# One hybrid layer on one core: the delta-rule phase issued in a TensorE order that the kernel's source works out

## The chip, the core and the metric

The kernel runs on one core of a Trainium2 chip. A core has a matrix engine (TensorE; PE in the profile, with its weight loads as PEld), VectorE (DVE), ScalarE (ACT), GpSimd (POOL) and SyncE (SP), each with an instruction stream of its own that it works off in order; semaphores connect them. SBUF is the working memory with 128 partitions; PSUM takes TensorE's results and has eight banks of 128 x 512 fp32. The metric is the time of one execution on the device, in microseconds (us). Of the kernel before, three runs took 1362.74, 1362.84 and 1366.62 us, so the median is 1362.84 us.

## The reference

512 tokens of width 1024 go through one layer with two mixing branches and an MLP. The first branch is the gated delta rule (8 heads, keys of 128, values of 256):

```
xn = rmsnorm(x); proj = xn @ w_in
q, k, v = split(silu(causal_depthwise_conv(proj[qkv], conv_a)))      # 4 taps over time
q = l2norm(q) / sqrt(128); k = l2norm(k); beta = sigmoid(.); g = -exp(a_log) * softplus(. + dt_bias)
# per head and chunk:
decay  = exp(g_cum[i] - g_cum[j])  for i >= j, else 0
lower  = strict_lower((k * beta) k^T * decay);  T = inverse(1 + lower)
attn   = (q k^T) * decay
v_new  = T (v * beta) - T (k * beta * exp(g_cum)) @ state
o      = (q * exp(g_cum)) @ state + attn @ v_new
state  = state * exp(g_last) + (k * exp(g_last - g_cum))^T @ v_new
ya = (rmsnorm(o, norm_a) * silu(z)) @ w_br_a
```

The second branch is chunked retention (rotary q and k, fixed decays, a silu gate, `w_br_b`). Both are gated and summed, go through `w_out`, and the MLP `square(relu(x @ w_up)) @ w_down` follows, with an rmsnorm before and after each part.

## The kernel before

All large products are fp32-accurate by splitting: a weight block `raw` of 128 x 1024 is loaded by SP (`weights`, L88), ACT rounds it to `whi` (L117), VectorE forms `wlo = raw - whi` (L118), and TensorE does three products for each pair of tiles: whi·xhi, whi·xlo, wlo·xhi (`mm3`, L84 to L86). One such product is a matmul of 128 x 128 by 128 x 512 (512 columns streamed). A "product" below is a group of these that fills one or more PSUM banks: `feature_major` (L252, features on partitions) and `token_major` (L272).

The delta-rule phase (L545 to L954) handles 8 heads in four pairs `g2`, with chunks of 128 tokens (the reference's 64-token chunks give the same function). Its pieces:

- `keys(g4)` (L683), four heads at a time: product K, then `conv_silu` (L630): ACT copies PSUM to `c_raw` (L635) and makes the first tap (L640), VectorE adds three taps (L642), ACT does tanh (L643), VectorE the last multiply (L646). TensorE transposes the result to token rows (`to_tokens`, L649), ACT sums squares (L657). `decays` (L659) makes the 128 x 128 decay tile: eight ACT scalings of a triangle (L665), two TensorE products against the constant matrix `later` (L666), one exp (L668). It is called for every head twice, once in `keys` and once in `values_queries`. Gram products k·kᵀ (L710) are scaled into `mt` (L713, which lies in `acc`), and `kd` is scaled (L716).
- `base_inverse(g4)` (L720): the 32 x 32 diagonal blocks of 16 matrices are rearranged through DRAM (L726, L732) onto 64 partitions and inverted there by 31 steps of a VectorE multiply (L741) and subtract (L747), each on at most 256 elements; results go back through DRAM (L749 to L753). It runs twice, for the two groups of heads.
- `double_blocks` (L758): four levels of small TensorE products that grow inverses from 32 to 128, called four times for 8 matrices each.
- `values_queries(g2)` (L804): products V and Q, convolutions, `vt` (L811), the attention tiles `at` (L830, L832), masked on POOL (L836).
- `recurrence(g2)` (L846): for four chunks in order: ks (L862), the correction (L865), px (L871), `vn` by ACT (L875), pc (L880), the new state (L885/L890), qs (L894), its scaling (L896), po (L901), the sum (L903). Each step takes one of three PSUM banks of the tag `dl`.
- `gated(g2)` (L927): product Z, tanh (L604), two VectorE multiplies (L605, L607); `gated_features` (L609) transposes the gated rows through the one PSUM bank of the tag `tr`; `ya_partial` (L671) multiplies by `w_br_a`.

The order on every engine is made when the program is built: a scheduler with a cost model takes instructions in program order and priority (`high_priority` moves them ahead). What `keep_in_program_order` marks stays in the order of the source. In the kernel before that is true of a part of the start and of the second branch's `token_product` (L242); the delta-rule products are free, and the scheduler mixes them. `add_blocks` (L158) puts DRAM-to-DRAM additions for later weights on POOL's queue, and `copy_block` puts copies on SP's.

## Time and profile before

| | |
|---|---|
| median of 3 runs | 1362.84 us |
| profiled execution, first to last instruction | 1362.5 us |
| start (norm of x, first keys) | to about 42.5 us |
| delta-rule phase | 42.5 to 485.5 us |
| second branch and its gates | to about 960 us |
| mixing and MLP | to the end |

The phases' bounds are read from the trace's timeline: the first product of the second group of keys starts at 42.57 us, the last sum of `ya_partial(2)` (L678) at 485.3 us. In the profile a TensorE instruction's start is exact and its end is modelled, so that neighbours overlap in the rows: the distance from one start to the next is what an instruction takes of the engine. An fp32 product that is not split shows as two records.

### The profile page before, as it was taken

What the parts mean: (1) busy time and instruction counts of PE and PEld (TensorE: products, weight loads), DVE (VectorE), ACT (ScalarE), POOL (GpSimd) and SP (SyncE); (2) the same over time, 40 slices, a digit from 0 to 9 for tenths busy, and PEclk for the clock granted to TensorE, in tenths of its full rate; (3) what the DMA queues carried; (4) which work ended last, traced back from release to release, by engine and by line L of the source; (5) the groups of instructions that cost most, each with busy time, mean ns of one, the idle gap of its engine ahead of it and who ended that gap; (6) DMA issues with size and microseconds to landing.
All of it is one profiled execution on the core that took longest, in us unless ns stands there. A gap on an engine that the chain in (4) does not pass through costs nothing.

```text
span 1362.5 us, 17876 instructions
## 1 busy us (share of the span) xinstructions
PE 1347.0 (99%) x6685; PEld 1110.7 (82%) x6685; DVE 912.8 (67%) x1606; ACT 651.7 (48%) x1204; POOL 109.4 (8%) x161
## 2 busy tenths in 40 slices
PE   9999999999999999999999999999999999999997
PEld 7888787788877888888888888888889888888886
DVE  5799899864665557567477577575775744828535
ACT  5977564624543322453453343343355736436441
POOL 2010310121011002000000100011101100000000
PEclk9999999999999999999999999999999999999999
DMA  5254715379458447775584782488639843625421
GB/s 178 64 154 133 202 43 180 117 153 238 108 124 169 110 147 158 190 240 193 131 255 132 192 263 93 154 217 182 199 117 238 224 154 110 197 95 169 132 86 62
DMA packets 101718, 214.70 MB, mean 158 GB/s; under 512 B 7158, under 2 KB 20624, under 8 KB 101120
## 3 DMA queue, kind: packets, MB, share of 16 engines
q1 hardware_dynamic: 85616, 170.41, 39.1%
q0 software_dynamic: 15280, 42.03, 17.0%
q8 instruction: 52, 0.85, 0.3%
q10 hardware_dynamic: 736, 1.12, 0.2%
q14 instruction: 34, 0.28, 0.1%
HBM read 207.77 MB, written 64.49 MB: 200 GB/s over the span
## 4 chain that ended last, share of the span: by engine, by line
PE 89%; DVE 5%; DMA 2%; ACT 2%; issue 1%; DVEq 0%; ACTq 0%
PE mm L84 18%; PE mm L85 18%; PE mm L86 18%; PE mm L242 10%; PE dl L242 10%; PE tr L323 3%; PE mm L456 2%; DVE wlo L118 1%; PE dl L86 1%; PE dl L85 1%; PE dl L84 1%; PE dl L901 1%; PE dl L871 1%; DVE c_y L642 1%; PE dl L880 1%; PE dl L862 1%
## 5 line engine op out<-in xcount | busy, mean ns | idle before, releaser
L118 DVE TENSOR_TENSOR wlo<-raw,whi 128x1024 fp32r<-128x1024 f32 x245 | 298.8, 1221 | 269.0 <-ACT whi L117 267.7
L117 ACT CAST whi<-raw 128x1024 fp32r<-128x1024 f32 x245 | 257.4, 1052 | 428.9 <-PE mm L85 243.4
L84 PE MATMUL mm<-actT,whi 128*128 128x512 f32 x480 | 190.1, 396 | 0.0
L85 PE MATMUL mm<-actT,whi 128*128 128x512 f32 x480 | 189.9, 396 | 0.0
L86 PE MATMUL mm<-actT,wlo 128*128 128x512 f32 x480 | 189.0, 395 | 0.0
L84 PEld LDWEIGHTS mm<-actT,whi 128*128 128x128 f32 x480 | 90.2, 188 | 18.7 <-ACT c_y L640 0.8
L86 PE MATMUL mm<-hn,wlo 128*128 128x512 f32 (+1 forms) x288 | 105.4, 366 | 0.0
L85 PE MATMUL mm<-hn,whi 128*128 128x512 f32 (+1 forms) x288 | 105.3, 366 | 0.0
L84 PE MATMUL mm<-hn,whi 128*128 128x512 f32 (+1 forms) x288 | 105.3, 366 | 0.0
L86 PEld LDWEIGHTS mm<-actT,wlo 128*128 128x128 f32 x480 | 90.3, 188 | 17.9
L85 PEld LDWEIGHTS mm<-actT,whi 128*128 128x128 f32 x480 | 90.3, 188 | 17.8
L84 PE MATMUL mm<-og,whi 128*128 128x512 f32 x256 | 99.7, 390 | 1.0 <-DVE zz L605 1.0
L85 PE MATMUL mm<-og,whi 128*128 128x512 f32 x256 | 99.6, 389 | 0.0
L86 PE MATMUL mm<-og,wlo 128*128 128x512 f32 x256 | 99.6, 389 | 0.0
L242 PE MATMUL mm<-whi,xsum 128*128 128x512 f32 x256 | 80.8, 389 | 0.0
L642 DVE SCALAR_TENSOR_TENSOR c_y<-c_raw,convw,c_y 128x512 f32<-128x512 f32 x96 | 69.7, 743 | 2.4 <-ACT c_y L640 1.8
L85 PEld LDWEIGHTS mm<-hn,whi 128*128 128x128 f32 x288 | 54.3, 189 | 8.8
L84 PEld LDWEIGHTS mm<-hn,whi 128*128 128x128 f32 x288 | 54.3, 189 | 8.7
L86 PEld LDWEIGHTS mm<-hn,wlo 128*128 128x128 f32 x288 | 54.3, 189 | 8.7
L84 PE MATMUL mm<-whi,actT 128*128 128x512 f32 x152 | 61.1, 402 | 0.1
L242 PE MATMUL dl<-whi,actT 128*128 128x512 f32 x192 | 61.1, 389 | 0.0
L242 PE MATMUL dl<-whi,ffq 128*128 128x512 f32 x192 | 61.0, 389 | 0.0
(345 smaller groups left out, 2608.8 us busy)
## 6 DMA issues: line engine op xcount, KB each, us to landing
raw<-in_w_in_dram SPq DMA_DIRECT2D x101, 512.0 KB, 4.3
raw<-sums SPq DMA_DIRECT2D x56, 512.0 KB, 4.2
raw<-in_w_up_dram SPq DMA_DIRECT2D x36, 512.0 KB, 4.6
sums<-in_w_in_dram SPq DMA_DIRECT2D x32, 512.0 KB, 5.6
sums<-sums POOLq DMA_DIRECT2D x28, 512.0 KB, 7.1
raw<-in_w_down_dram SPq DMA_DIRECT2D x26, 512.0 KB, 3.8
sums<-in_w_down_dram SPq DMA_DIRECT2D x24, 512.0 KB, 7.4
raw<-in_w_br_a_dram SPq DMA_DIRECT2D x16, 512.0 KB, 4.0
```

The costliest lines, as they stand in the source:

```text
L84: nc.tensor.matmul(ps, lh, rh, start=first, stop=False)
L85: nc.tensor.matmul(ps, lh, rl, start=False, stop=False)
L86: nc.tensor.matmul(ps, ll, rh, start=False, stop=last)
L117: nc.scalar.copy(hi[:, :n], raw[:, :n])
L118: nc.vector.tensor_tensor(lo[:, :n], raw[:, :n], hi[:, :n], ALU.subtract)
L242: m = nc.tensor.matmul(pss[t], lhs[i // 2], rhs[i % 2], start=first and k + i == 0, stop=k + i == 5, skip_group_check=not first,)
L323: nc.tensor.transpose(ps, src, ident)
L456: nc.tensor.matmul(ps[:, ts], ws[w][:, kk, f * P : (f + 1) * P], xs[x][:, k, ts], start=first and kk + i == 0, stop=kk == len(ks) - 1 and ...
L642: nc.vector.scalar_tensor_tensor(y, raw[:, j : j + T], tap(j), y, ALU.mult, ALU.add)
L862: nc.tensor.matmul(ks[:, hh, :], kf[:, h0 + hh, cs], state[:, hh, :], start=True, stop=True)
L871: nc.tensor.matmul(px[:, hh, :], rt[:, nn[hh], :], vx[:, hh, :], start=True, stop=True)
L880: nc.tensor.matmul(pc[:, hh, :], kd[:, nn[hh], :], vn[:, hh, :], start=True, stop=True)
```

## The change

The arithmetic of the layer stays; the delta-rule phase is rewritten.

1. **Order.** A class `Clock` adds up assumed TensorE times. Each piece is a generator; `run` steps those that are due by this clock and fills the rest with units of three 512-column matmuls from a list of large products. All TensorE instructions of the phase are pinned in that order.
2. **Decays once.** Cumulated g goes as 32 rows to DRAM and comes back broadcast over 128 partitions; POOL masks it, ACT makes 32 exps into `dall`, which `keys` and the attention tiles both use (and which the attention tiles then replace).
3. **Convolution from PSUM.** The copy to `c_raw` is left out; the taps read PSUM. Values and queries take one ACT `Silu` in place of tanh and a VectorE multiply. The gates take `Silu` too, also in the second branch.
4. **Inverse once.** All 32 matrices on 128 partitions, moved by VectorE block transposes in place of DRAM; each step's two operations are cut in two halves. All keys come before it, and doubling runs for all four groups level by level.
5. `kd` is no longer scaled: ACT writes px twice, scaled by `brd` and by `br`. qs moves next to ks, and the state is updated in place.

```diff
+SMALL_US, CONV_US, TOK_US, PK_US, INV_US, DB_US = 10.5, 6.5, 2.5, 2.0, 62.0, 0.5
+VT_US, KS_US, PX_US, PC_US, GATE_US, ... = 2.5, 2.4, 3.5, 2.4, 11.0, ...
+# INV_PRIO 0, CONV_PRIO 600, SMALL_PRIO 800, KEY_PRIO 600, DECAY_US 20.0, AHEAD 700
...
+    class Clock:
...
+        def matmul(self, *args, **kwargs):
+            m = tc.keep_in_program_order(nc.tensor.matmul(*args, **kwargs))
...
+            if args[1].dtype == F32R:
+                self.now += 0.0135 + n / 2400
+            else:
+                self.now += 0.006 + 4 * n / 2400
...
+        def run(self, fillers):
...
+                due = [c for c in self.chains if self.ready(c[0]) <= self.now]
+                if due:
+                    self.step(min(due, key=lambda c: self.ready(c[0])))
+                    continue
...
+                        if all(self.events.get(n, float("inf")) <= self.now for n in f[1]):
+                            fillers.remove(f)
+                            current = f[0]()
+                            break
...
+        clock.matmul(pg[0:32, 2, :], gf, tri, start=True, stop=True)
...
+        nc.gpsimd.dma_start(g_d, g_rows)
...
+            nc.gpsimd.dma_start(gb.rearrange("p n t -> p (n t)"), rows.partition_broadcast(P))
+            nc.gpsimd.affine_select(gb, gb, pattern=[[0, 16], [1, P]], ...)
...
+                        nc.scalar.activation(
+                            dall[:, 4 * h + c, :], gb[:, 4 * i + c, :], AF.Exp, bias=neg_g[:, c, h : h + 1]
...
+            clock.done(f"decay{g4}", DECAY_US + 5 * g4)
...
-        nc.scalar.copy(raw[:, 3 : T + 3], ps)
...
+                nc.vector.scalar_tensor_tensor(y[:, s:T], ps[:, 0 : T - s], tap(j), y[:, s:T], ALU.mult, ALU.add)
+            if th is None:
+                with tc.issue_after(exps[-1].ins):
+                    nc.scalar.activation(y, y, AF.Silu, scale=2.0)
...
+        def base_inverse():
+            yield "mt0"
+            yield "mt1"
...
+                    cuts = (0, (nr + 1) // 2, nr) if nr > 3 else (0, nr)
...
+            clock.done("inverse", INV_US)
...
+                    qs = chain_bank()
+                    for hh in range(2):
+                        clock.matmul(qs[:, hs[hh], :], qf[:, hh, cs], state[:, hs[hh], :], start=True, stop=True)
+                    yield KS_US - (clock.now - t1)
...
+                    for w, scale in ((vx, brd), (vn, br))[c == 3 :]:
+                        for hh in range(2):
+                            nc.scalar.activation(w[:, hs[hh], :], px[:, hs[hh], :], AF.Copy, scale=scale[:, nn[hh] : nn[hh] + 1])
+                yield PX_US
...
+        def delta_chain():
+            yield "inverse"
+            yield from double_blocks()
+            for g2 in range(4):
+                for f in range(4):
+                    yield f"v{g2}{f}"
+                yield f"q{g2}"
+                yield from recurrence(g2)
+                clock.start(gate_chain(g2))
...
+                (second_keys_filler, ()),
+                (value_filler(0), ()),
+                (query_filler(0), ()),
+                (gate_filler(0), ()),
+                (value_filler(1), ()),
+                (query_filler(1), ()),
+                (ya_filler(0), ("og0", "doubled")),
+                (value_filler(2), ("og0",)),
+                (query_filler(2), ("og0",)),
+                (gate_filler(1), ("gate0",)),
...
```

At the start, half of the first keys' products for the second 256 tokens move ahead of the second half of the small product (beta and g), pinned. `AHEAD` raises the priority of weight splits within the phase.

## The prediction

> **What bounds the kernel now.** I read the page first, then the stretches before and after 485.5 us, then TensorE's waits, then the chain of waits, and last the groups on VectorE and ACT.

> ```profile
> span 1362.5 us, 17876 instructions
> PE 1347.0 (99%) x6685; PEld 1110.7 (82%) x6685; DVE 912.8 (67%) x1606; ACT 651.7 (48%) x1204; POOL 109.4 (8%) x161
> ```

> ```profile
> 42.50:485.50 443.00, 437.72 (x2411) 354.10 (x2410) 325.84 (x730) 238.62 (x587) 57.18 (x96) 1.00 0.54 138
> 485.50:560.00 74.50, 74.50 (x343) 61.77 (x342) 53.65 (x66) 26.48 (x33) 9.21 (x11) 1.00 0.67 163
> 600.00:625.00 25.00, 25.00 (x112) 20.68 (x112) 19.50 (x27) 13.22 (x21) 0.00 (x0) 1.00 0.95 306
> ```

> ```profile
> 578.23 5.44 PE dl L242 x24
> ```

> A matmul of 512 columns takes 5.44 / 24 = 0.227 us, and a 25 us stretch that touches 112 of them is full. After the delta-rule phase TensorE is saturated, and only work taken from it shortens the time there. So everything is decided in the 443.0 us of the phase. Its TensorE work, by start-to-start distances:

> ```profile
> 42.50:485.50 443.00, 178.55 (x449) 84.24 (x449) 1.00 0.54 138
> 42.50:485.50 443.00, 12.08 (x32) 5.63 (x32) 1.00 0.54 138
> 42.50:485.50 443.00, 28.23 (x180) 20.76 (x180) 1.00 0.54 138
> 171.69 1.03 PE L894 MATMUL dl<-st,qf 128*128 128x256 f32 x4
> 172.55 1.03 PE L901 MATMUL dl<-vn,at 128*128 128x256 f32 x4
> 98.20 0.60 PE L323 MATMUL tr<-cmat,qf 128*128 128x128 f32 x4
> 98.64 1.06 PE L830 MATMUL dl<-qf,kf 128*128 128x128 f32 x8
> 99.45 0.71 PE L666 MATMUL dl<-tg,later 128*128 128x512 f32 x2
> 100.00 0.39 PE L84 MATMUL mm<-actT,whi 128*128 128x512 f32 x1
> 158.60 1.07 PE dl L797 x16
> 184.86 1.09 PE L780 MATMUL dl<-rn,acc 32*32 32x32 f32 x32
> ```

> The first row is L84 alone; L85 and L86 have 448 each, so 1345 x 0.227 = 304.9. Decays (second row): 32 x 0.227 = 7.3. Transposes (third row): 180 x 0.11 = 19.8. Recurrence: 272 records at 0.86 / 4 = 0.215, 58.6. Gram and attention: 128 at 0.81 / 8 = 0.101, 13.0. Doubling: 128 records at 0.067 and 320 at 0.032, 18.8. Sum 422.4, so some 20 us of 443.0 are not work. The order can win no more than that. The view of TensorE's waits in the phase has six rows of one wait each, 5.0 us together (first two and last):

> ```profile
> PE dl L880 <- ACT vn L875: 1.2, 1, 1.2
> PE tr L594 <- issue: 1.1, 1, 1.1
> ...
> PE dl L666 <- DVE acc L713: 0.5, 1, 0.5
> ```

> The other 15 are short breaks, mostly at changes between kinds of matmul.

> **The change, part by part.**

> *Decays once.* Gone are 32 products of 0.227 us, 7.3, and the breaks around 16 pairs of them. From 99.45 to 100.00 a pair takes 0.55 us instead of 0.453, so 0.1 each, 1.6. One cumulative product is added, 0.2. Net -8.7 us of TensorE. ACT loses the 128 scalings:

> ```profile
> L665 ACT ACTIVATE tg<-cmat,ghi 128x128 fp32r<-128x128 f32 x64 | 22.5, 403 | 0.3 <-PE dl L666 0.3
> L836 POOL TENSOR_SCALAR_AFFINE_SELECT at<-at 128x1024 f32<-128x1024 f32 x4 | 7.6, 1892 | 27.2 <-DVE ssq L842 15.6 <-DVE at L832 11.6
> ya_d<-acc POOLq DMA_DIRECT2D x2, 1024.0 KB, 9.3
> vecs_in<-in_norm_b_dram POOLq DMA_DIRECT2D x1, 8.0 KB, 2.2
> ```

> The new path is longer: 2.2 us for a small transfer, up to 9.3 for 1 MB, 2 x 1.89 for a mask of twice the size, 16 exps of 0.403: 21.7 us to the first half, where the planner says 20; the second half, with one more mask and 16 exps, about 32 against 25. The second keys and first values (192 matmuls, 43.5 us) cover it. Without that cover the Gram scalings, and behind them the inverse, are late by up to 7 us. Two queues get a new wait. On POOL the mask waits for the broadcast; behind it stand only the inverse's memsets, which need the keys anyway. On ACT the exps wait for the mask; behind them stand weight splits, and three split blocks are held at a time, each good for 24 matmuls or 5.4 us, so a hold-up of up to 10 us stays covered. The first values' taps write into the tile that the broadcast used, so V's first two PSUM banks are held until the last exp; the other two take its second half. I take 0 for all of it; bounds 0 and 7.

> *Convolution, gates, kd.*

> ```profile
> L642 DVE SCALAR_TENSOR_TENSOR c_y<-c_raw,convw,c_y 128x512 f32<-128x512 f32 x42 | 30.4, 742 | 0.5 <-ACT c_y L640 0.5
> L605 DVE SCALAR_TENSOR_TENSOR zz<-zz,mm 128x512 f32<-128x512 f32 x16 | 10.8, 678 | 0.3 <-ACT zz L604 0.3
> ```

> VectorE loses the last multiply (L646; like L605 over 512 elements, 0.68 us) for 24 tiles, 16 gate multiplies (L605), 32 kd scalings and one of two inverses; ACT loses 30 copies. Both only feed TensorE, so I book nothing. A tap from PSUM is not in the trace; the nearest rows are L605, which reads PSUM, at 0.678 and L642, all in SBUF, at 0.742: bounds 0.68 and 0.74 a tap, and I keep 0.74. Gone with the inverse are POOL's transfers for it (L726 to L765); the block additions on that queue stay 10 and 12 in the phase. In the second branch 16 VectorE multiplies go; TensorE is full there: 0. Table loads for `Silu` lie on ACT, at 48%: 0, and a few us if each met a wait. The start is reordered between products that stood close to each other: 0, plus or minus 1.

> [...]

> *The pinned order.* It replaces the order in which the six waits stood. All six lie at places where the new order puts products between, so -5.0; none of the 15 us of breaks is booked, since each chain step is still a visit between large products. At best a third, 5, goes too; at worst they grow by as much.

> *Inverse once, late.* This is the part that can cost. TensorE has work before the first recurrence: K, V, Q, Z, V, Q are 480 matmuls, 108.8 us; 80 transposes 8.8; Gram and attention 9.7; doubling 18.8: 146 us. VectorE's work in the same time:

> ```profile
> L118 DVE TENSOR_TENSOR wlo<-raw,whi 128x1024 fp32r<-128x1024 f32 x17 | 20.7, 1218 | 9.5 <-ACT whi L117 9.3
> L713 DVE SCALAR_TENSOR_TENSOR acc<-dl,br,dt 128x128 f32<-128x128 f32 x32 | 10.9, 344 | 0.0
> L747 DVE TENSOR_TENSOR mrb<-mrb,tmp 64x31 f32<-64x31 f32 (+15 forms) x31 | 10.2, 330 | 0.1
> L741 DVE TENSOR_TENSOR tmp<-mrb 64x31 f32<-64x31 f32 (+15 forms) x31 | 10.2, 328 | 0.1
> L748 DVE COPY mrb<-mrb 64x1024 f32<-64x1024 f32 x1 | 1.1, 1131 | 0.0
> L782 DVE COPY y<-dl 32x256 f32<-32x256 f32 x8 | 3.4, 424 | 3.6 <-PE dl L780 3.5
> L303 DVE SCALAR_TENSOR_TENSOR rs_y<-rs_t,rs_y 128x8 f32<-128x8 f32 (+1 forms) x30 | 4.9, 163 | 0.6
> 85.66 2.06 DVE L642 SCALAR_TENSOR_TENSOR c_y<-c_raw,convw,c_y 128x512 f32<-128x512 f32 x3
> ```

> 40 splits 48.7; 20 convolutions of three taps, eight with the last multiply of 0.68, 50.0; Gram scalings, rescaled values and attention 19.2; the inverse 20.4, some 4 for its halves (an estimate: the 62 more instructions at the 0.07 us that neighbours leave between them) and 11 block transposes at 1.1 (not in the trace; nearest row L748), 36.5; doubling's 28 copies at 0.42 (L782) to 0.69, 14; some 50 small operations at 0.16 (L303), 8: 176. Three taps took 2.06 us rather than 2.23, so VectorE delivers it in 176 x 0.92 = 163 us. That is 17 more than TensorE's 146. But V and Q of the second pair, 19.5 x 0.92 = 18 of it, are not needed by the first recurrence and can follow the inverse. So TensorE waits between 0 and 17 us at the first doubling product; I take 2.5, nearer to 0 since the work that can stand back is as large as the gap.

> *Recurrence 0 without cover.* The next products wait for its gated rows (`og0`, `gate0`), and the six above are used up. Before, it ran so:

> ```profile
> 163.75 1.02 PE L871 MATMUL dl<-vt,rt 128*128 128x256 f32 x4
> 165.34 1.13 PE L880 MATMUL dl<-vn,kd 128*128 128x256 f32 x4
> 183.91 1.03 PE L901 MATMUL dl<-vn,at 128*128 128x256 f32 x4
> 172.75 0.84 ACT L896 ACTIVATE vt<-dl,eg 128x256 f32<-128x256 f32 x2
> ```

> From 163.75 to 184.8 are 21.0 us, of which 17 groups of 0.86 are its own, 14.7: 6.3 us that other products filled before and nothing must fill now. The second pair's queries leave a few pieces there, so 3.0; bounds 0 and 6.3.

> Sum, on the profiled execution: 1362.5 - 8.7 - 5.0 + 2.5 + 3.0 = 1354.3; the median stands 0.3 above the span, 1354.6 us. Its own range: 1354.6 - 2.5 - 3.0 - 5 = 1344 with nothing late and a third of the breaks gone; 1354.6 + 3.3 + 2 = 1360 with recurrence 0 bare and the inverse a little late.

> **Rivals.**

> *The inverse becomes the bound (slower).* Place: the first doubling product. Convolutions and splits carry priority 600 and 700, the inverse 0; if VectorE does all of V and Q first, the whole 17 us are waited, and recurrence 0 behind it is bare: 1354.6 + 14.5 + 3.3 = 1372. It decides against the change once the wait passes 2.5 + 8.2 = 10.7 us. For it: VectorE was that full while the first inverse ran before (48.97 of 50 us, the row below). Against it: the planner leaves 62 us for the inverse, and the rows give 36.5 for it alone.

> ```profile
> 100.00:150.00 50.00, 48.95 (x254) 39.65 (x253) 48.97 (x143) 39.05 (x116) 9.17 (x15) 1.00 0.58 174
> ```

> *po waits for a bank (no change).* With qs held from ks on, po of chunks 1 and 2 may get the bank of qs. Its scaling writes where pc reads, so it starts after pc (0.86), takes 0.84 and a hand-over: about 1.1 us of waiting in eight places, 8.8: 1363. For it: three banks and five tiles for each chunk. Against: px's bank is free by then, if the scheduler takes that one.

> *The planner's clock doesn't fit (slower).* Its latencies are fixed, and a pinned TensorE cannot step aside as the free order could. With some 110 visits, 0.15 us more at each is 16: 1354.6 + 16 = 1371. Against: most of its gaps are longer than the rows ask (3.5 us where px to pc took 1.59, from 163.75 to 165.34).

> **How the numbers follow.** Forecast 0.54, inverse 0.22, bank 0.14, clock 0.10. About 0.3%, 4 us, can be told from no change. The forecast is faster by that except at its upper end (0.04 within): faster 0.50. Within: 0.04, plus 0.12 of the bank rival: 0.16. Slower: the rest, 0.34. The range starts at 1344 and reaches into both slow cases, to 1374; above lies what stalls in both ways at once.

> **What would show it.** Right: no L666 rows; TensorE's waits in the phase under 10 us; the phase's end near 477 instead of 485.5; waits concentrated at the first doubling and the first recurrence. Wrong: a wait of over 10 us at doubling behind VectorE's inverse; eight waits at po behind ACT's scaling of qs; a TensorE idle share spread over all transposes; or times after 485.5 us that differ, which nothing here explains.

## The result and the profile after

The changed kernel takes 1387.24 us (median of four runs, 1373.68 to 1398.07) against 1363.67 us; the ratio is 1.0088, with a 95% interval of 1.0061 to 1.0115: slower, where faster was forecast. This ratio and those below leave out runs over 1.5% above the fastest of the same kernel, here the two above 1395 us, whose mean granted clock was 0.977 and 0.979. The profiled run has 1373.68 us and a span of 1371.9. Its page begins:

```profile
span 1371.9 us, 17419 instructions
PE 1346.9 (98%) x6655; PEld 1111.1 (81%) x6655; DVE 879.5 (64%) x1491; ACT 608.9 (44%) x1085; POOL 81.5 (6%) x91
```

TensorE is busy for as long as before (1347.0), although 32 products are gone. VectorE and ACT lost 33 and 43 us. Two of the stretches shown of before, now after (start and end, length, then busy time and count of PE, PEld, DVE, ACT and POOL, granted clock, DMA share, GB/s), with two of 25 us inside the phase:

```profile
42.50:485.50 443.00, 429.85 (x2376) 354.51 (x2376) 302.33 (x641) 199.73 (x474) 30.52 (x30) 0.99 0.53 135
600.00:625.00 25.00, 25.00 (x111) 20.49 (x110) 17.17 (x22) 13.15 (x21) 0.00 (x0) 1.00 0.96 296
100.00:125.00 25.00, 21.49 (x92) 17.36 (x91) 23.53 (x47) 8.15 (x11) 2.85 (x3) 0.93 0.78 203
150.00:175.00 25.00, 20.81 (x139) 16.34 (x137) 24.00 (x21) 7.68 (x10) 2.87 (x3) 0.86 0.90 224
```

Two stretches stand out: TensorE stands still for 3.5 and 4.2 us while VectorE is full, and the granted clock is below 1.00, which it was in none of the stretches shown of before. The first product of the second branch marks the end of the phase; from the timeline, before and then after:

```profile
578.07 0.39 PE L242 MATMUL dl<-whi,actT 128*128 128x512 f32 x1
```

```profile
577.64 0.39 PE L244 MATMUL dl<-whi,actT 128*128 128x512 f32 x1
```

So the phase gained 0.4 us where 8 were forecast, and the part behind it, which the change hardly touches, lost 9.8 (1371.9 - 577.6 against 1362.5 - 578.1). A second profile of each kernel (e0_before and e0_after below) gives 576.48 and 578.37, so the phase's 0.4 is uncertain by one or two microseconds; the loss behind it, 11.6 there, is not in doubt. These are two separate questions.

**Inside the phase.** TensorE's waits there (what waited, for what, us in all, times, longest):

```profile
PE tr L583 <- ACT vt L806: 4.4, 2, 4.2
PE dl L583 <- ACT vt L806: 3.5, 1, 3.5
PE dl L574 <- ACT vt L1094: 1.6, 2, 1.0
PE dl L574 <- ACT vn L1094: 0.9, 2, 0.6
```

All rows of this view add up to 13.0 us; before it was 5.0.

The two long waits stand at token transposes of V, at 109.6 and 158.9 us, and the releaser is the Silu of V. ACT was not late itself: its input was. VectorE's timeline ahead of the first wait (start, duration), a little shortened:

```profile
97.98 0.75 DVE L803 SCALAR_TENSOR_TENSOR vt<-mm,convw,vt 128x511 f32<-128x511 f32 x1 [0.26 <-ACT vt L800]
98.65 2.03 DVE L908 STREAM_TRANSPOSE mrb<-acc 32x1024 f32<-32x1024 f32 x1
100.62 0.69 DVE L803 SCALAR_TENSOR_TENSOR vt<-mm,convw,vt 128x510 f32<-128x510 f32 x1
101.34 2.02 DVE L908 STREAM_TRANSPOSE mrb<-acc 32x1024 f32<-32x1024 f32 x1
...
105.96 2.03 DVE L908 STREAM_TRANSPOSE mrb<-acc 32x1024 f32<-32x1024 f32 x1
108.02 0.75 DVE L803 SCALAR_TENSOR_TENSOR vt<-mm,convw,vt 128x510 f32<-128x510 f32 x1
108.80 1.97 DVE L908 STREAM_TRANSPOSE mrb<-acc 32x1024 f32<-32x1024 f32 x1
110.80 1.22 DVE L120 TENSOR_TENSOR wlo<-raw,whi 128x1024 fp32r<-128x1024 f32 x1
111.94 0.74 DVE L803 SCALAR_TENSOR_TENSOR vt<-mm,convw,vt 128x509 f32<-128x509 f32 x1
```

Between V's taps stand the inverse's block transposes, at 2.0 us each and not at the 1.1 that the prediction took. The groups of all eleven:

```profile
L908 DVE STREAM_TRANSPOSE mrb<-acc 32x1024 f32<-32x1024 f32 x4 | 8.0, 2012 | 0.1
L933 DVE STREAM_TRANSPOSE rt<-mrb 32x1024 f32<-32x1024 f32 x4 | 7.8, 1956 | 0.1
L929 DVE STREAM_TRANSPOSE rn<-mrb 32x1024 f32<-32x1024 f32 x3 | 7.0, 2324 | 0.1
```

22.8 us instead of 12.1. What the waits are followed by is seen in windows cut to the trace's record of the granted clock:

```profile
110.00:114.20 4.20, 0.74 (x6) 0.70 (x7) 3.91 (x5) 0.63 (x1) 2.01 (x2) 1.00 0.60 98
114.20:117.60 3.40, 3.40 (x10) 2.64 (x9) 2.62 (x6) 1.51 (x2) 0.00 (x0) 0.50 1.03 149
117.60:121.00 3.40, 3.40 (x16) 2.77 (x15) 3.37 (x11) 0.80 (x3) 0.00 (x0) 0.99 0.97 190
158.00:162.00 4.00, 1.31 (x6) 0.75 (x4) 3.90 (x5) 0.00 (x0) 0.00 (x0) 1.00 0.97 117
162.00:168.80 6.80, 5.30 (x15) 4.34 (x16) 6.74 (x9) 2.32 (x4) 0.35 (x1) 0.50 0.68 181
```

Behind each wait the clock is 0.50, for 3.4 and for 6.8 us: 10 matmuls in 3.4 us and then 16. At 0.50 two neighbours of 512 columns start 0.43 us apart (at 116.27 and 116.70), at 1.00 0.23. So the 3.4 us cost some 1.6 us more (an estimate: 3.4 x (1 - 0.23 / 0.43)), and here a wait of 3.5 us is paid about one and a half times.

**Behind the phase.** The same window in both kernels, before and then after:

```profile
1100.00:1340.00 240.00, 240.00 (x1060) 198.43 (x1058) 137.64 (x179) 113.25 (x163) 0.00 (x0) 1.00 0.39 127
```

```profile
1100.00:1340.00 240.00, 240.00 (x1039) 194.72 (x1038) 132.66 (x158) 111.59 (x153) 0.00 (x0) 1.00 0.41 129
```

TensorE is full and the clock is 1.00 in both, but one matmul takes 240 / 1039 = 231.0 ns in the mean instead of 226.4. Not all products slow down: by the distances of their starts behind the phase, those over `hn` go from 226.7 to 233.2 ns and those over `xsum` from 226.7 to 232.6, while those over `og` stay at 227.

### The profile page after: what moved, and what is told of

The parts are those of the page before. It is cut to its first block, busy times and chain, and to the rows that moved or that the text cites. A ratio compares the mean times of both kernels' runs of the same rounds, so it can differ in the third digit from the quotient of the medians.

```text
span 1371.9 us, 17419 instructions
## 1 busy us (share of the span) xinstructions
PE 1346.9 (98%) x6655; PEld 1111.1 (81%) x6655; DVE 879.5 (64%) x1491; ACT 608.9 (44%) x1085; POOL 81.5 (6%) x91
## 4 chain that ended last, share of the span: by engine, by line
PE 86%; DVE 7%; ACT 4%; DMA 2%; issue 1%; DVEq 0%; ACTq 0%; SPq 0%
PE mm L574 16%; PE mm L87 13%; PE mm L88 13%; PE mm L86 13%; PE mm L244 10%; PE dl L244 10%; PE dl L574 5%; DVE wlo L120 1%; PE dl L88 1%; PE tr L583 1%; PE dl L87 1%; PE dl L86 1%; DVE vt L803 1%; PE tr L324 1%; DMA raw<-in_w_in_dram 1%
## 5 line engine op out<-in xcount | busy, mean ns | idle before, releaser
L574 PE MATMUL mm<-actT,whi 128*128 128x512 f32 x448 | 147.0, 410 | 0.0
L86 PE MATMUL mm<-hn,whi 128*128 128x512 f32 (+1 forms) x288 | 106.6, 370 | 0.0
L86 PE MATMUL mm<-actT,whi 128*128 128x512 f32 x256 | 100.8, 394 | 0.0
L87 PE MATMUL mm<-actT,whi 128*128 128x512 f32 x256 | 100.2, 391 | 0.0
L574 PEld LDWEIGHTS mm<-actT,whi 128*128 128x128 f32 x448 | 82.0, 192 | 15.3
L574 PE MATMUL mm<-whi,actT 128*128 128x512 f32 x256 | 87.5, 408 | 0.4 <-DVE qf L803 0.4
L86 PEld LDWEIGHTS mm<-hn,whi 128*128 128x128 f32 x288 | 54.2, 188 | 10.2
L87 PEld LDWEIGHTS mm<-hn,whi 128*128 128x128 f32 x288 | 54.1, 188 | 10.2
L87 PE MATMUL mm<-og,whi 128*128 128x512 f32 x160 | 62.4, 390 | 0.0
L86 PE MATMUL mm<-og,whi 128*128 128x512 f32 x160 | 62.3, 390 | 0.0
L88 PE MATMUL mm<-og,wlo 128*128 128x512 f32 x160 | 62.3, 389 | 0.0
L244 PE MATMUL dl<-whi,ffq 128*128 128x512 f32 x192 | 61.4, 391 | 0.0
L574 PE MATMUL mm<-og,whi 128*128 128x512 f32 x192 | 60.6, 397 | 0.0
```

Of the source, the lines that this page charges most:

```text
L86: nc.tensor.matmul(ps, lh, rh, start=first, stop=False)
L87: nc.tensor.matmul(ps, lh, rl, start=False, stop=False)
L88: nc.tensor.matmul(ps, ll, rh, start=False, stop=last)
L244: m = nc.tensor.matmul(pss[t], lhs[i // 2], rhs[i % 2], start=first and k + i == 0, stop=k + i == 5, skip_group_check=not first,)
L574: m = tc.keep_in_program_order(nc.tensor.matmul(*args, **kwargs))
```

## Experiments: chip, transposes, waits

Two runs without an edit came first: the kernel before and the changed one, profiled in one session.

> The unchanged kernel of before, profiled in the same session as the changed one. In the profile of the changed kernel the phase ended 0.4 us early (first second-branch product at 577.64 against 578.07), yet the end came 9.4 us later, because the unchanged products after 577 us stood 229 to 233 ns apart instead of 227. If that pace belongs to the chip or the session, this kernel shows it too: some 230 ns in the stretch 1100 to 1350 us and a time of about 1370. If the change brings it, this kernel shows 227 ns there and 1363.

Measured: 1363.04 us and again 1060 matmuls in 1100 to 1340 us. The pace is not the session's.

> The changed kernel once more, beside the kernel before on the same chip. Theory: its two TensorE waits of 3.5 and 4.4 us at the token transposes of V (109.6 and 158.9 us) come back at the same places, and a stretch of granted clock 0.5 of 3 to 7 us follows each; ratio near 1.009. Rival (chip): the ratio comes out near 1.000 and no stretch of 0.5 stands in the middle of the trace.

Measured: ratio 1.0125 (1.0055 to 1.0195), waits of 3.5 and 3.9 us at the same places, stretches of 0.5 of 3.4 and 6.8 us behind them, 1039 matmuls in the window.

```diff
+                    nc.scalar.copy(flat[bs], mt[bs, :, bs])
+                nc.vector.transpose(mb.rearrange("p (c m) -> p c m", m=32), flat.rearrange("p n c -> p c n"))
...
+                nc.vector.transpose(flat.rearrange("p n c -> p c n"), rb3)
+                for b in (1, 3, 0, 2):
+                    nc.scalar.copy(rt[blocks[b], :, blocks[b]], flat[blocks[b]])
```

> The eleven 32-partition block transposes of the inverse become three of 128 partitions, with eleven block copies on ACT. Theory (VectorE's transposes at 2.0 us stand between V's taps, Silu of V is late, the pinned TensorE waits): VectorE loses some 16 us of its work up to the first recurrence, the waits at V's token transposes shrink from 3.5 and 4.4 us to under 1.5 each, no clock stretch of 0.5 follows, and the kernel gains the waits (6 us) and the half-clock time (5 us), 11 us in all, more if the pace of later products goes with the clock. If a 128-partition transpose takes four times as long, nothing is gained. Rival (the planner's fixed latencies are the cause anywhere): the waits move to other places and the sum stays.

Measured: ratio 1.0035 (0.9997 to 1.0072), ten runs from 1361.38 to 1380.74 (granted clock 0.983 to 0.999); profiled span 1360.1. The waits at V's tokens are 0.2 us and the second branch begins at 567.43: 10.2 us gained in the phase. The three transposes (line numbers are each kernel's own from here on):

```profile
L928 DVE STREAM_TRANSPOSE mrb<-mrb 128x1024 f32<-128x1024 f32 x1 | 2.3, 2270 | 0.0
L932 DVE STREAM_TRANSPOSE mrb<-mrb 128x1024 f32<-128x1024 f32 x1 | 2.1, 2108 | 1.5 <-ACT rn L931 1.5
L909 DVE STREAM_TRANSPOSE mrb<-rn 128x1024 f32<-128x1024 f32 x1 | 2.1, 2101 | 0.0
```

128 partitions took 2.1 to 2.3 us here, no more than the 2.0 to 2.3 of 32 partitions above. Later products stay slow (1039), with no clock of 0.5 anywhere before the end: the pace has another cause.

```diff
-            yield clock.vector(2.1, 0.9) + CONV_US
+            yield clock.vector(2.1, 0.9) + CONV_US + (5.0 if g2 < 2 else 0.0)
```

> The transposes stay as they are; the planner asks for V's token transposes of the first two pairs 5 us later, so other products stand in TensorE's order ahead of them. Theory: the two waits of 3.5 and 4.4 us fall to below 1 us, the clock stays at 1.0, and the gain is about that of the run with three transposes (8 to 11 us). If the products that come first wait themselves for VectorE (their weights are split there, their PSUM banks freed there), the waits only move: gain under 3 us.

Measured: ratio 1.0236 (1.0219 to 1.0254): the expectation failed. V's tokens no longer wait, but the doubling does: its copies stand behind the inverse's transposes and V's taps in VectorE's order. From TensorE's timeline, and the window cut to the clock's record:

```profile
175.72 1.70 PE L574 MATMUL dl<-rn,acc 32*32 32x32 f32 x32 [7.93 <-DVE mrb L952]
```

```profile
170.30:231.70 61.40, 55.42 (x443) 42.91 (x444) 28.63 (x48) 6.71 (x11) 3.97 (x4) 0.50 0.51 110
```

The same lateness, moved to the place that the prediction's first rival named, then 61.4 us at half clock.

```diff
-                    nc.vector.transpose(
+                    nc.vector.tensor_copy(
                         mb[bs].rearrange("p (c m) -> p c m", m=32), mt[bs, :, bs].rearrange("p n c -> p c n")
```

> The changed kernel with its eleven block transposes replaced by plain copies of the same blocks (the inverse is then computed from untransposed blocks: the values differ). The prediction priced a transpose as such a copy, 1.1 us; measured were 2.0. Theory (the price of the transposes makes the waits): the waits at V's tokens shrink from 3.5 and 4.4 us to about 1 or less, no stretch of clock 0.5 follows them, and the time is about 1361, as with three transposes. Rival (any work of the inverse between V's taps does it): waits of over 2.5 us each stay.

Measured: 1368.31 us in the profiled run, ratio 1.0141 (1.0073 to 1.0209) over all.

```profile
L933 DVE COPY rt<-mrb 32x1024 f32<-32x1024 f32 x4 | 4.4, 1097 | 0.0
L908 DVE COPY mrb<-acc 32x1024 f32<-32x1024 f32 x4 | 4.3, 1084 | 0.1
L929 DVE COPY rn<-mrb 32x1024 f32<-32x1024 f32 x3 | 3.7, 1246 | 0.1
```

At the predicted price the waits at V's tokens go (0.3 us), and the second branch begins at 569.68, 8.0 us earlier. A wait of 2.3 us at the first pair's gate products comes instead, with 3.4 us at half clock behind it, and three of four runs are at a clock of 0.98: the price explains the waits at V's tokens, not the whole time.

## Experiments: the place in SBUF

The removed tiles (a third of `cmat`, `later`, `ghi` or `glo`: 512 + 512 + 128 bytes a partition, and `sp_h` with 128 in the next pool) lay ahead of everything that comes later. So weight blocks moved by -1152 bytes and `hn` by -1280: by 128 against each other.

```diff
+    cp.tile([P, 288], F32, name="pad_c")
+    sm.tile([P, 32], F32, tag="pad_s", name="pad_s", bufs=1)
```

> The changed kernel with two unused tiles (1152 and 128 bytes a partition), so that every tile used after the phase lies at the address that it had before the change (the change had removed tiles in front of them: the stationary blocks moved by -1152 bytes, the moving hn by -1280). So far the products after 577 us stood 229 to 233 ns apart in all three runs of the changed kernel's layout, with and without a clock of 0.5, and 227 in both runs of the old layout. Theory (place in SBUF): 227 ns again between 1100 and 1350 us, the part after the phase shorter by 9 us, the two waits at V's tokens as before, so about 1364 in the runs with the shortest half-clock stretches. Rival (the pace goes with the engines' work or the order after the phase): still 229 to 233 ns and 1373.

> Three transposes of 128 partitions and the two unused tiles together. Three transposes alone ended at 1360.1 us with the clock at 1.0 throughout and the later products at 229 to 233 ns. Theory (two separate causes that add): 1360 - 9 = 1351, faster than before by 0.8%; later products 227 ns apart. Rival (one cause): no better than 1360.

> The kernel before with one unused tile of 128 bytes a partition ahead of the phase's and the second branch's tiles: stationary blocks stay where they were, hn and the sums move by 128 bytes. Nothing else changes. Theory (the relative place of the operands in SBUF sets the pace): the products over hn come to 229 ns or more, and the kernel is slower by up to 9 us. Rival (place makes no difference, or only a shift of the stationary blocks does): 227 ns and 1363.5.

> The kernel before with one unused tile of 128 bytes a partition ahead of all others: hn, the sums and the stationary blocks all move by the same 128 bytes. With hn alone moved (e6_before_sm) the products over hn came to 229 to 233 ns and the kernel lost 8.7 us. Theory (it is the place of the operands to each other that counts): 227 ns between 1100 and 1350 us, 1363. Rival (the place of hn itself, 160 modulo 256 instead of 32): 229 to 233 ns, 1372.

The last two add only the second, or only the first tile (with 32 in place of 288) to the kernel before. Measured, with the window 1100 to 1340 of e5, e6 and e7 below:

| kernel | moved against each other | matmuls in 240 us | time, us | ratio |
|---|---|---|---|---|
| e4 | 0 | 1059 | 1367.36 to 1390.40 | 1.0102 (1.0040 to 1.0165) |
| e5 | 0 | 1060 | 1352.58 to 1373.10 | 0.9954 (0.9929 to 0.9980) |
| e6 | +128 bytes | 1039 | 1371.52 to 1374.47 | 1.0065 (1.0047 to 1.0083) |
| e7 | 0 (both moved) | 1060 | 1365.53 (one run) | |

```profile
1100.00:1340.00 240.00, 240.00 (x1060) 198.42 (x1059) 136.62 (x183) 110.50 (x163) 0.00 (x0) 1.00 0.39 123
```

```profile
1100.00:1340.00 240.00, 240.00 (x1039) 194.66 (x1038) 133.05 (x158) 111.96 (x154) 0.00 (x0) 1.00 0.41 129
```

```profile
1100.00:1340.00 240.00, 240.00 (x1060) 198.39 (x1059) 137.81 (x177) 113.74 (x162) 0.00 (x0) 1.00 0.40 127
```

An unused tile of 128 bytes slows the kernel before by 8.9 us (0.0065 of 1363.75); one that moves everything does not. Of this, 7.7 us lie behind the phase (from the first product of the second branch to the end, 793.4 us in e6 and 785.7 in e7). So the relative place counts. Between e2 and e5 the profiled span falls from 1360.1 to 1351.8, 8.3 us, of which 7.6 lie behind the phase (792.7 against 785.1). The 1351 expected of e5 is what four of its nine runs come near (1352.58 to 1354.11); its median is 1359.47. In e4 the pace comes back, but its times lie no better than the changed kernel's within their spread: what the pads give, the clock takes in those runs (in its profile, 47.8 us at half clock from 179.0 us on). Only the distances 0 and 128 bytes were tried, and why the products stand further apart at 128 stays open.

## Experiments: the clock and the order

e5 still has a standstill of 1.8 us between two gate products at 115.5 us, and its runs differ with the clock (0.983 to 0.999). The next kernels move the inverse behind the first pair's query taps, whole (e8) or its steps alone (e11), and free TensorE's order.

```diff
+                with tc.issue_after(taps[-1].ins):
+                    nc.vector.transpose(mb.rearrange("p (c m) -> p c m", m=32), flat.rearrange("p n c -> p c n"))
```

> Three transposes and pads as in e5_three_pads, and the inverse's first transpose is issued after the last tap of the first pair's queries. In e5 one wait of 1.4 us stood at 115.5 us (a start-to-start distance of 1.80): the first pair's gate products needed the bank that the taps behind the inverse's first steps read; runs of one and the same program lay between 1352.6 and 1373.1 with granted clocks of 0.999 to 0.983. Theory (a stretch of clock 0.5 follows when TensorE stands still for about 2 us or more, and 1.8 is at the edge): without this wait all runs lie at 0.998 or above and within 1350 to 1355, median 1351. Rival (the clock falls for another reason, the load itself): some runs still fall to 0.99 or below.

Measured: twelve runs from 1354.46 to 1386.07 (median 1369.25), clocks 0.974 to 0.999, ratio 0.9986 (0.9959 to 1.0014). The expectation failed: the wait at 115.5 went, and came back as 2.5 us at V's tokens of the second pair and 4.2 us in recurrence 0, behind the inverse's copies on ACT.

```diff
-            m = tc.keep_in_program_order(nc.tensor.matmul(*args, **kwargs))
+            m = nc.tensor.matmul(*args, **kwargs)
```

> e8_inverse_behind with TensorE's matmuls and transposes of the phase left free to be ordered by the scheduler (the order in the source stays as its starting point). The prediction booked -5.0 us for the pinned order and +3.0 for recurrence 0 without cover. If both hold, the free order is slower by 5 us where chain steps stand, but puts products of the first pair's gates into recurrence 0 and wins up to 3 there: between +2 and +5 us against e8. Rival (a pinned TensorE cannot step aside and the free order has what it needs): faster than e8 by 1 to 3 us, and the waits between px and pc in recurrence 0 (1.0, 0.6, 0.6 us) go.

Measured: ratio 1.0013 (0.9981 to 1.0045), best runs 1353.86 to 1354.34. The waits of recurrence 0 are gone, but a wait of 2.1 us at V's tokens stays, and eight of twelve runs stand at a clock of 0.977 to 0.981. The median, 1369.13, is that of e8: neither of the two expected differences shows through the clock.

```diff
+                for i2 in range(2):
+                    clock.matmul(pd, xs[0][:, i2, 0:P], xs[0][:, i2, :], start=i2 == 0, stop=i2 == 1)
                 pk = psx.tile([P, 4, P], F32, tag="dl", name="dl", bufs=3)
```

> e8_inverse_behind with two products of 512 columns (their result is not used) put back ahead of each of the eight Gram groups: half of the 32 decay products that the change took away. The prediction priced them at 0.227 us each and 0.1 for the breaks around a pair: 8 x 0.55 = 4.4 us slower than e8. If VectorE sets the pace there (the keys' part of the phase), less than 2 us.

The whole time (1.0096, 1.0067 to 1.0125) is clouded by the clock, so I read it up to the first gate product, where both have 1.00; e8 and then e10:

```profile
111.46 0.40 PE L576 MATMUL mm<-whi,actT 128*128 128x512 f32 x1
```

```profile
115.74 0.40 PE L576 MATMUL mm<-whi,actT 128*128 128x512 f32 x1
```

That is 4.28 us for half of the products; 4.4 was predicted.

```diff
+                            if j == 0:
+                                behind.enter_context(tc.issue_after(taps[-1].ins))
```

> e5_three_pads with the inverse's elimination steps (not its first transpose) issued after the last tap of the first pair's queries. Deferring the transpose too (e8_inverse_behind) took the wait of 1.4 us at 115.5 away, but put the inverse's ACT copies and transposes in front of the second pair's taps (2.5 us at 158) and of recurrence 0 (4.2 us at 199), and the clock fell after both. Here the steps move by 2 us only. Theory (a stretch of clock 0.5 follows a standstill of TensorE of about 2 us or more, and nothing else): no start-to-start distance above 1.6 us in the phase, all runs at a clock of 0.997 or above, median 1351 to 1353. If the clock still falls below 0.99 in some runs while the profile shows no standstill above 1.6 us, the rule is wrong or the standstills differ from run to run.

Measured: six runs from 1365.49 to 1379.25, all at a clock of 0.979 to 0.987, ratio 1.0072 (1.0043 to 1.0100). The rule fell: the longest standstill up to there is 1.41 us (at 168.1), and the stretch of 0.5 lasts 44.4 us, from the doubling on.

```profile
170.20:214.60 44.40, 44.40 (x347) 34.51 (x344) 16.75 (x30) 4.03 (x6) 6.01 (x6) 0.50 0.69 122
```

> The same with TensorE's order in the phase left free. In e9_free_order the three waits between px and pc of recurrence 0 were gone and its undisturbed runs lay at 1354, the same as e8's. Theory (a free order costs nothing in the pieces and covers recurrence 0): 1 to 3 us faster than e11_steps_behind at the same clock. Rival (pinning is worth the 5 us that the prediction booked): 3 to 5 us slower.

> e5_three_pads with the free order alone. The wait of 1.4 us at 115.5 us stays, since the scheduler's order parts from the planner's only behind the doubling. Theory: the undisturbed runs at 1349 to 1351 (recurrence 0 covered, 1 to 3 us), about half of the runs with a clock below 0.997 as in e5.

e12 is e11, e13 is e5, each with the order left free. Measured: e12 0.9911 (0.9896 to 0.9927), 1348.46 to 1354.24, clocks 0.996 to 0.999; e13 0.9925 (0.9900 to 0.9949), nine of ten runs below 1354, clocks 0.984 to 0.999. Both beat the kernel before; e12 by 0.9%, the lowest ratio of this study, though the interval of e13 overlaps with it. At a clock of 1.00 throughout the phase, the second branch begins in e5 and e13 at:

```profile
566.71 0.39 PE L244 MATMUL dl<-whi,actT 128*128 128x512 f32 x1
```

```profile
561.04 0.39 PE L244 MATMUL dl<-whi,actT 128*128 128x512 f32 x1
```

The pinned order costs 5.7 us, more than the 1 to 3 expected. The waits account for 4.3 of it: all rows of the view of TensorE's waits in the phase add up to 6.6 us in e5 and 2.3 in e13, and 2.5 of the difference stood behind px in recurrence 0. The wait at 115.5 us, which was expected to stay, fell from 1.4 to 0.8. What the free one does with the gap between px and pc of recurrence 0 shows in the timelines of e5 and then e13:

```profile
208.67 1.03 PE L576 MATMUL dl<-vt,rt 128*128 128x256 f32 x4
210.26 1.13 PE L576 MATMUL dl<-vt,kd 128*128 128x256 f32 x4 [0.56 <-ACT vt L1097]
```

```profile
207.52 1.03 PE L576 MATMUL dl<-vt,rt 128*128 128x256 f32 x4
208.19 0.58 PE L576 MATMUL mm<-wlo,actT 128*128 128x512 f32 x1
208.61 0.63 PE L576 MATMUL mm<-whi,actT 128*128 128x512 f32 x2
209.11 1.13 PE L576 MATMUL dl<-vt,kd 128*128 128x256 f32 x4
```

The last run takes up why the clock falls for so long in e11:

```diff
                 ps = psx.tile([P, T], F32, tag="dl", name="dl", bufs=3)
+                for i in range(3):
+                    clock.matmul(ps, xs[0][:, i, 0:P], xs[0][:, i, :], start=i == 0, stop=i == 2)
```

> e11_steps_behind with three products of 512 columns (their result is not used) ahead of each of the sixteen groups of the doubling. In e11 no standstill was longer than 1.41 us, yet the clock of all six runs fell to 0.979 to 0.987; in its profile the stretch of 0.5 began at 170.2 us and lasted 44.4 us. Long stretches (44 to 61 us) began in four profiles, all between 168 and 174 us, where the doubling stands: 448 products of 32 or 64 rows and columns in 33 us. Theory (it is the small products, which keep little of the array busy, that let the clock fall for so long): with 48 full products among them the long stretch is gone, all runs at 0.995 or above, and in spite of 10.9 us of added work the kernel is faster than e11 (1374): about 1352 + 11 = 1363. Rival (the stretch comes from the wait or from elsewhere): clocks of 0.98 as before and 1374 + 8 = 1382 or more.

Measured: eleven runs from 1362.43 to 1366.01, clocks 0.997 to 0.999, ratio 1.0002 (0.9993 to 1.0011): 48 products more, 10.9 us of work, and 10 us faster than e11 (medians 1363.67 and 1374.03). The times and clocks are as the theory had them, but the run doesn't show that the small products alone are the cause. Every kernel with the new order gathers the same 448 small products, in some sixteen groups with 45 full products between them (90 in e15), and eight of the thirteen profiles without e15's products show no long stretch. The doubling of e12, then of e15:

```profile
159.40:191.90 32.50, 32.50 (x502) 25.63 (x501) 22.70 (x41) 7.93 (x10) 3.72 (x4) 1.00 0.77 141
```

```profile
160.20:204.10 43.90, 43.26 (x547) 34.05 (x546) 23.76 (x41) 5.15 (x7) 6.90 (x7) 1.00 0.85 174
```

e12 kept a clock of 0.996 or more in six of six runs without the added products. And e15 changed a second thing: the standstill of 1.41 us inside the doubling became 0.91. A standstill there is the rival that stays, though its size alone doesn't decide either: e9 lost the clock in the doubling with standstills of 0.73 and 0.85 us, e15 kept it with 0.91.

The profiles hold five long stretches, one more than the expectation counted: 61.4 us in e3, 44.4 in e10 and e11, 47.8 in e9 and, from 179.0 us on, in e4. All five begin while the doubling stands and end 2.5 to 6.3 us after its last small product. So in these five the clock, once fallen inside the doubling, stayed low until the small products were through; what made it fall is open. Before the change the small products were spread from 148.6 to 294.4 us, and the clock there was 1.00 in its profiles.

## Why the prediction was wrong

| step | predicted | measured |
|---|---|---|
| Decays once | -8.7 | 4.28 for half (e10 against e8): -8.6 |
| Convolution from PSUM | 0, tap 0.74 | tap 0.74 (row below); no wait of its own |
| The pinned order | -5.0 | waits 6.6 us in e5, 5.0 before; free, the order is 5.7 better still |
| Inverse once, late | +2.5 | waits of 3.5 + 4.2 = 7.7, and half clock behind them; e2 takes back 10.2 |
| Recurrence 0 without cover | +3.0 | waits of 1.6 + 0.9 = 2.5 |
| behind the phase | 0 | +9.8; the place in SBUF is 7.6 of it (e2 against e5) |

```profile
L803 DVE SCALAR_TENSOR_TENSOR vt<-mm,convw,vt 128x511 f32<-128x511 f32 x16 | 11.9, 741 | 6.6 <-ACT vt L800 5.3 <-issue 1.2
```

*Decays once, Convolution, Recurrence 0* hold to half a microsecond, as far as these rows show. The tap that reads PSUM takes 741 ns (L803, the row above), what the SBUF tap took before (L642, 742 ns in the prediction's row).

*The pinned order* took waits away from their old places, but not for the reason and not by the sum that were booked. It is not the pinning: in e12 and e13, which leave the order free, all waits add up to 2.2 and 2.3 us. In e5, pinned, they add up to 6.6 us against 5.0 before, so e5 won nothing in the waits. Its phase is 11.4 us shorter than before. The decays are 8.6 of that; the remaining 2.8 and the 1.6 us of added waits must have come out of the short breaks, for which the prediction booked 0 and allowed 5 either way. No run separates this part, and two profiles of the kernel before differ by 1.6 us at the phase's end. Freed, the same order gains 5.7 us more, in part since the scheduler may put gate products between px and pc. The rival "the planner's clock doesn't fit" was right that a pinned TensorE cannot step aside, but priced it as 0.15 us at 110 visits; it was mainly two waits of 3.5 and 4.2 us. The bank rival's eight waits at po are not among the rows.

*Inverse once, late* is the step that failed inside the phase, in three ways. Its size: a block transpose was priced by L748, a copy, at 1.1 us, and took 2.0 to 2.3. Its place: the prediction let VectorE's ledger end at the first doubling product; but the scheduler had dealt the transposes out between V's taps, and a pinned TensorE met V's tokens first (e3 shows the wait at the doubling once V gives way). And a term was missing: each of the two waits is followed by a stretch of half clock. In place of 2.5 us stood 7.7 of waits and what the clock took; shorter transposes gave 10.2 back (e2). The sign "TensorE's waits in the phase under 10 us" says the same: they were 13.0. That the profiled 1371.9 us lies beside the first rival's 1372 is luck: 9.8 of the 17.6 us between it and the forecast span of 1354.3 come from behind the phase, where that rival changed nothing.

"Times after 485.5 us that differ, which nothing here explains" named the sign of the second failure. The step that let it in is the sum itself: it counted instructions, and took it that the products kept their pace of 0.227 us when tiles ahead of them disappeared.

With both repaired and the order as in the change (e5), the profiled span is 1351.8 against the 1354.3 of the sum. That is a run whose clock held; the median of e5 is 1359.47.

## What to carry to other kernels

Price an operation that the trace does not show by an experiment or by wide bounds, and look for its first victim in the static order of the engine that it lands on, not at the end of a ledger. Here a wait on TensorE cost more than its length where the clock followed it (3.5 us and some 1.6 by the estimate above), and where the small products were gathered in one place a fall of the clock lasted until they were through (44.4 us in e11): read the granted clock at such places in several runs, not in one profile. Leave the order free where something else is ready. When untouched code changes its pace, compare where its operands lie before looking for contention.

## What the runs showed of the hardware

```profile
425.00:450.00 25.00, 24.13 (x105) 19.71 (x106) 12.82 (x27) 13.19 (x35) 4.26 (x5) 0.93 0.60 119
```

```profile
PE dl L881 <- ACT vn L876: 2.0, 1, 2.0
```

And in e11 the clock fell in the doubling with no standstill over 1.41 us. The traces give no single limit: waits of 1.4 (e5) and 1.5 us (e0_before) have no stretch behind them and the 2.0 us of e6 has one, but after the 2.1 us of e9 the clock stayed at 1.0 until the doubling. What else decides it was not measured.

**Block transposes** of 1024 fp32 elements a partition took 2.0 to 2.3 us each on VectorE with 32 partitions (the changed kernel) and 2.1 to 2.3 with 128 (e2).

**Operands in SBUF.** In the changed kernel, with `hn` moved by 128 bytes against the weight blocks, the products over `hn` stood 233.2 ns apart and those over `xsum` 232.6, against 226.7 for both before. In e6, where only `hn` and the sums are moved, 576 products over `hn` take 134.88 us of the window 1100 to 1340, as in the changed kernel, and the part behind the phase is 7.7 us longer than in e7. Moved together with the blocks (e7) they take 131.05 us, as before the change.
